# Head sums of a hybrid decoder layer: split in two halves over all rows, or fp32 in four strips and spread through DRAM

## The chip, the core and the metric

The kernel runs on one core of a Trainium2 chip. The metric is the device time of one execution in microseconds (us). One matmul instruction multiplies a stationary operand (at most 128 x 128) with up to 512 moving columns.

## The reference

One layer for 1088 tokens (1024 of a prompt and 8 sequences of 8), model width 1024. A projection of the normalised input gives the columns of two branches. The branch that matters here is RWKV-7: 512 channels are 8 heads of 64.

```python
kk = heads(k * lp["k_k"])
kk = kk * lax.rsqrt(jnp.sum(kk * kk, axis=-1, keepdims=True) + 1e-12)
...
y, wkv_new = wkv7_scan(wkv_prev.astype(f32), rh, heads(decay), kh, vh, kk, ah)
mean = jnp.mean(y, axis=-1, keepdims=True)
var = jnp.mean(jnp.square(y - mean), axis=-1, keepdims=True)
y = ((y - mean) * lax.rsqrt(var + GN_EPS)).reshape(B, T, MIX_WIDTH)
y = y * lp["ln_w"].astype(f32) + lp["ln_b"].astype(f32)
bonus = jnp.sum(rh * kh * lp["r_k"].astype(f32), axis=-1, keepdims=True) * vh
y = (y + bonus.reshape(B, T, MIX_WIDTH)).astype(pr.dtype) * g
```

Four sums run over the 64 channels of a head for each token: that of the key, the bonus, the mean and the variance. The branch is gated, projected, merged with a pooling branch, projected again and added to the input; a squared-ReLU MLP of width 4096 follows.

## The kernel before

Features lie on the partitions and the 1088 tokens along the free axis, so a unit f (0 to 3) of 128 partitions holds two heads. A sum over a head is a sum over 64 partitions: a matmul with a constant 128 x 128 matrix of two blocks of ones (`bones`), which gives the sum on all 64 rows of the head at once.

Two phases. In the first, a long stream of matmuls (the input projection, then the pooling branch's output projection, `op_job`) fills TensorE. Each product is made of three fp32r matmuls, high by high, high by low and low by high, in chunks of 364, 362 and 362 columns (tiles `whi`, `wlo` for weights, `hx` for rows). Beside the stream run generators: `heads` (line 1650), which takes the four units one after the other, `chains`, `pools` and `or_rows`. `heads` does for each unit:

- `front` (1112): squares the key, sums it over the head, takes the inverse root, and makes decays and keys;
- `scores`, then `inverse`, `level` and `affine`: small matmuls and VectorE work;
- beside these `bonus` (1214) of this unit, and `post` (1561) of the unit before: group norm (mean, variance), bonus and gate. `post` of the last unit has no unit behind it and runs at the end, in pieces; it uses plain fp32 matmuls with the constant in `kct`.

The second phase begins with `or_job` (1900), which multiplies the rows that all four `post` calls have left; its first products need those of `post(3)`.

Before each step a generator yields `need(...)`: it goes on when the planner's own clock (`Clocks`, line 80, fed with a modelled cost of each operation) says that the operands are there. This writes TensorE's order down once and for all. `Ledger` (184) then sets the order of VectorE and of SP's queue from a second model. Every engine takes its instructions in that order and waits for semaphores.

A head sum outside the last `post` is taken so: `halves` splits the row into a high part (ScalarE, a copy to fp32r) and a low part (VectorE, a subtraction), `sums` multiplies both with `bones` into one PSUM bank, chunk by chunk (512, 288, 288 in `front`, 364, 362, 362 elsewhere). `rinv` and `inv` add epsilon and take a reciprocal of all the chunk's columns on VectorE, with the root on ScalarE. Rows are tiles `wt`, a ring of five.

Of the kernel before, what the change touches and what calls it, by code (L numbers as in the profile page):

```python
# [183 lines left out]
class Ledger:  # L184
# [44 lines left out]
    def product(self, shape, n, dtype):  # L229

        if dtype == F32R:
            return n / 2.4 + 14
        if shape == (32, 32):
            return 22
        if max(shape) <= 64:
            return max(58, 0.78 * n + 11)
        if shape == (128, 32):
            return 0.47 * n
        if shape == (128, 128):
            return max(207, 1.62 * n + 60)  # L240
        return max(58, 1.05 * n)
# [302 lines left out]
class K:  # L544
# [42 lines left out]
    def took(self, n, mode):  # L587
        if not self.clocks.on:
            return max(n / 0.6 * min(mode) / 128, 30) + 3
        if mode == (64, 128):  # L590
            return n + 10
        if mode == (64, 64):
# [238 lines left out]
    def inv(self, ps, n, out, scale, eps):  # L831
        nc = self.nc
        nc.scalar.activation(out, ps[:, :n], AF.Identity, bias=self.eps[:, eps:eps + 1], scale=scale)
        for a in range(0, n, 182):
            nc.vector.reciprocal(out[:, a:min(a + 182, n)], out[:, a:min(a + 182, n)])

# [275 lines left out]
    def front(self, f):  # L1112
# [14 lines left out]
        hi, lo = (self.row(self.p1, "wt", 5, F32R) for _ in range(2))  # L1127
        for c0, n in FH:
            self.halves(kk[:, c0:c0 + n], hi[:, c0:c0 + n], lo[:, c0:c0 + n])
        for c0, n in FP:  # L1130
            yield self.need(hi[:, c0:c0 + n], lo[:, c0:c0 + n], wait=0)
            self.rinv(self.sums(hi[:, c0:c0 + n], lo[:, c0:c0 + n]), n, kk[:, c0:c0 + n], 1.0, 1)
        t1, tha = self.wt(hi), self.wt(lo)
        for c0, n in FP:
# [6 lines left out]
            nc.scalar.activation(tha[:, c0:c0 + n], ps[:, :n], AF.Tanh, bias=self.hp[:, 4 + f:5 + f], scale=0.5)  # L1141
        yield X(f)
# [43 lines left out]
        q = [self.wt(x, F32R) for x in (t1, tha)]  # L1186
        self.halves(k, *q)
        v = self.wt(k)
        nc.sync.dma_start(v, self.d_x[8 + f])
        self.cur.update(q=q, v=v)  # L1190
# [23 lines left out]
    def bonus(self, f, d):  # L1214

        nc, (hi, lo), v, bv = self.nc, d["q"], d["v"], self.wt(d["kk"])
# [344 lines left out]
    def post(self, f):  # L1561
# [57 lines left out]
        else:  # L1619
            hi, lo = (self.row(self.p1, "wt", 5, F32R) for _ in range(2))  # L1620
            for c0, n in CH:
                self.halves(y[:, c0:c0 + n], hi[:, c0:c0 + n], lo[:, c0:c0 + n])
            for c0, n in CH:
                s = slice(c0, c0 + n)
                yield self.need(hi[:, s], lo[:, s], wait=0)
                nc.vector.scalar_tensor_tensor(y[:, s], self.sums(hi[:, s], lo[:, s]), -1.0 / 64, y[:, s], op0=ALU.mult, op1=ALU.add)
                nc.scalar.activation(sq[:, s], y[:, s], AF.Square)
                self.halves(sq[:, s], hi[:, s], lo[:, s])
            yield self.need(hi, lo, wait=0)
            for c0, n in CH:  # L1630
                s = slice(c0, c0 + n)
                yield self.need(hi[:, s], lo[:, s], wait=0)
                self.inv(self.sums(hi[:, s], lo[:, s]), n, sq[:, s], 1.0 / 64, 2)
            nc.scalar.activation(sq, sq, AF.Sqrt)
            for c0, n in CH:
                s = slice(c0, c0 + n)
                nc.vector.tensor_tensor(y[:, s], y[:, s], sq[:, s], op=ALU.mult)
                nc.scalar.activation(y[:, s], y[:, s], AF.Identity, bias=self.par("ln_b", f), scale=self.par("ln_w", f))
            yield self.need(y[:, 0:1], banks=(), wait=0)
            bv, sg = yield from gate(sq, hi)  # L1640
# [62 lines left out]
    def run(self):  # L1703
        tc, nc, io = self.tc, self.nc, self.io
        with ExitStack() as ctx:
# [3 lines left out]
            dp = ctx.enter_context(tc.tile_pool(name="dp", bufs=1, space=DRAM))  # L1709
# [799 lines left out]
```

## Time and profile before

| | us |
|---|---|
| runs (3), median | 1580.98 (1580.57 to 1582.55) |
| profiled execution, its own time | 1581.41 |
| its span, first to last instruction | 1579.6 |
| TensorE busy | 1529.0 (97%) |
| VectorE busy | 1106.4 (70%) |
| ScalarE busy | 661.6 (42%) |

TensorE is busy nearly all the time; the time before its first matmul is about 9 us. In the rows below, PE is TensorE, DVE VectorE, ACT ScalarE, SPq the queue of DMAs that SyncE issues. A matmul row gives its start, its length with the pipeline's fill, and how many instructions it merges; an fp32 matmul leaves two records, an fp32r matmul one. Matmuls overlap, so their price is read from start to start.

### The profile page before, as it was taken

To read this page: it belongs to the slowest core of one execution; us is meant where nothing else is said; L and a number is where in the kernel's file an instruction comes from. 1 tells how busy PE (TensorE), PEld (TensorE's weight loads), DVE (VectorE), ACT (ScalarE), POOL (GpSimd) and SP (SyncE) were. 2 spreads that over 40 slices of the span, in tenths; PEclk is the share of its full clock that TensorE was granted. 3 is DMA by queue.
4 is the path that set the end of the run, shared out by engine and by line. 5 is a ranking of instruction groups with operands and counts; after the bars stand their busy time and mean duration, and the time that the engine had idled before them with its cause. 6 is when DMAs were issued, how large, how long until landed. Compare 5 with 4: busy or idle time off the path is not lost.

```text
span 1579.6 us, 34105 instructions
## 1 busy us (share of the span) xinstructions
PE 1529.0 (97%) x13822; PEld 1430.2 (91%) x13822; DVE 1106.4 (70%) x1945; ACT 661.6 (42%) x1294; POOL 141.4 (9%) x231
## 2 busy tenths in 40 slices
PE   6999899999999999999999999999999999999997
PEld 2998788887898889888899999999999999999997
DVE  5486568777777658546535798999667796666776
ACT  5554364365336434423223572222334344334552
POOL 2100100000000000113401210000000050000000
PEclk9999999999999999999999999999999999999999
DMA  9242524344324334854875565665436996664754
GB/s 368 83 124 94 187 65 122 106 124 136 109 86 154 104 125 145 311 184 173 307 272 183 183 200 182 228 232 178 150 139 238 391 356 196 203 197 156 229 171 152
DMA packets 136493, 290.04 MB, mean 184 GB/s; under 512 B 36976, under 2 KB 41072, under 8 KB 136336
## 3 DMA queue, kind: packets, MB, share of 16 engines
q1 hardware_dynamic: 129952, 266.75, 49.3%
q10 hardware_dynamic: 4320, 14.00, 2.5%
q0 software_dynamic: 2064, 7.13, 1.4%
q8 instruction: 108, 1.77, 0.5%
q14 instruction: 49, 0.40, 0.1%
HBM read 210.54 MB, written 77.28 MB: 182 GB/s over the span
## 4 chain that ended last, share of the span: by engine, by line
PE 58%; DVE 5%; DMA 4%; ACT 1%; issue 1%; POOL 0%; SPq 0%; DVEq 0%; ACTq 0%; POOLq 0%
PE mm L581 38%; PE wc L581 12%; PE w L581 8%; DVE wt L400 2%; DMA mg<-in_w_ff 1%; DVE hx L400 1%; DVE wlo L400 1%; DMA wt<-d_bv 1%; DMA hid<-in_w_ada_mlp 1%; DVE mg L400 0%; DMA wt<-d_x 0%; DVE hv L400 0%; ACT wt L400 0%; POOL t L400 0%; DMA t<-d_th 0%
## 5 line engine op out<-in xcount | busy, mean ns | idle before, releaser
L581 PE MATMUL mm<-hx,whi 128*128 128x362 f32 (+2 forms) x2944 | 687.8, 321 | 7.1 <-ACT px L400 2.7
L581 PEld LDWEIGHTS mm<-hx,whi 128*128 128x128 f32 x2944 | 495.3, 189 | 29.2 <-issue 8.0
L581 PE MATMUL mm<-hx,wlo 128*128 128x362 f32 (+2 forms) x1472 | 462.1, 314 | 2.4 <-issue 2.4
L581 PEld LDWEIGHTS mm<-hx,wlo 128*128 128x128 f32 x1472 | 278.4, 189 | 3.8 <-issue 3.5
L581 PE MATMUL mm<-mg,whi 128*128 128x272 f32 (+2 forms) x1312 | 248.7, 288 | 0.2 <-ACT t L400 0.2
L581 PEld LDWEIGHTS mm<-mg,whi 128*128 128x128 f32 x1312 | 205.4, 188 | 4.8 <-issue 2.5
L581 PE MATMUL mm<-mg,wlo 128*128 128x272 f32 (+2 forms) x656 | 188.5, 287 | 0.0
L581 PE MATMUL wc<-hx,whi 128*128 128x272 f32 x896 | 170.5, 288 | 0.0
L400 ACT ACTIVATE whi<-hid 128x512 fp32r<-128x512 f32 x128 | 80.4, 630 | 150.1 <-PE mm L581 54.9
L581 PEld LDWEIGHTS wc<-hx,whi 128*128 128x128 f32 x896 | 140.3, 188 | 0.2 <-issue 0.2
L581 PE MATMUL wc<-hx,wlo 128*128 128x272 f32 x448 | 128.9, 288 | 1.8 <-DVE wlo L400 1.8
L581 PEld LDWEIGHTS mm<-mg,wlo 128*128 128x128 f32 x656 | 123.5, 188 | 0.0
L400 DVE TENSOR_TENSOR wlo<-hid,whi 128x512 fp32r<-128x512 f32 x128 | 87.4, 686 | 45.2 <-ACT whi L400 44.3
L400 DVE TENSOR_TENSOR wlo<-wraw,whi 128x512 fp32r<-128x512 f32 x84 | 59.5, 709 | 61.2 <-ACT whi L400 61.0
L581 PE MATMUL w<-hx,whi 128*128 128x272 f32 (+1 forms) x480 | 98.1, 298 | 1.6 <-ACT hx L400 1.5
L400 ACT ACTIVATE whi<-wraw 128x512 fp32r<-128x512 f32 x100 | 62.5, 627 | 66.5 <-PE mm L581 24.2
L400 POOL TENSOR_TENSOR hx<-hx,rs 128x64 f32<-128x64 f32 x24 | 36.5, 1523 | 565.9 <-DVE rs L400 556.6
L581 PEld LDWEIGHTS wc<-hx,wlo 128*128 128x128 f32 x448 | 84.2, 188 | 2.2 <-DVE wlo L400 2.2
L581 PEld LDWEIGHTS w<-hx,whi 128*128 128x128 f32 x480 | 77.7, 189 | 3.0 <-ACT hx L400 1.8
L581 PEld LDWEIGHTS mm<-mg,hx 128*128 128x128 f32 x576 | 72.8, 188 | 5.0 <-issue 5.0
L581 PE MATMUL mm<-mg,hx 128*128 128x272 f32 (+2 forms) x576 | 74.7, 289 | 0.0
L581 PE MATMUL w<-hx,wlo 128*128 128x272 f32 (+1 forms) x240 | 70.7, 296 | 0.8 <-DVE wlo L400 0.8
(292 smaller groups left out, 2277.7 us busy)
## 6 DMA issues: line engine op xcount, KB each, us to landing
t<-d_t SPq DMA_DIRECT2D x56, 544.0 KB, 5.1
hid<-in_w_ff SPq DMA_DIRECT2D x110, 256.0 KB, 4.1
d_t<-hx SPq DMA_DIRECT2D x102, 272.0 KB, 2.2
hid<-in_w_ff SPq DMA_DIRECT2D x42, 512.0 KB, 3.9
wraw<-in_w_in SPq DMA_DIRECT2D x68, 256.0 KB, 2.9
mg<-in_w_ff SPq DMA_DIRECT2D x58, 256.0 KB, 5.3
hid<-in_w_ada_mlp SPq DMA_DIRECT2D x24, 512.0 KB, 5.9
d_th<-px SPq DMA_DIRECT2D x22, 544.0 KB, 3.1
```

The source lines that it names most:

```text
L400: r = f(*a, **kw)
L581: r = self.nc.tensor.matmul(out, lhsT, rhs, **kw)
```

## The change

All head sums but those of `post(3)` are taken in fp32 from the row itself. `strips` cuts the 1088 columns in four strips of 272. For each strip one matmul with 32 columns of `bones` (16 of each head) writes 32 partitions of one bank, at four places of the array. The result, 128 x 272, goes through ScalarE (with root and scale, or copied), for key and variance through one VectorE reciprocal of 272 columns; then `fan` stores every 16th partition (8 x 272) to DRAM and loads it back twice, broadcast to the 64 partitions of each head, over the row that was summed. The splits, and the loops over chunks around the sums, are gone; the element-wise work after the mean runs over whole rows. Two modelled costs are added for the planner.

```diff
+    def strips(self, x):
+        n = x.shape[1] // 4
+        ps = self.ps("w")
+        for i in range(4):
+            self.mm(ps[32 * i:32 * i + 32, :n], self.kc("bones")[:, 48:80], x[:, i * n:(i + 1) * n], start=True, stop=True, tile_position=(0, 32 * i))
+        return ps[:, :n]
+    def invert(self, x, eps, scale):
+        nc, r = self.nc, x[:, :HALF // 2]
+        nc.scalar.activation(r, self.strips(x), AF.Sqrt, bias=self.eps[:, eps:eps + 1], scale=scale)
+        nc.vector.reciprocal(r, r)
+        self.fan(x)
+    def fan(self, x):
+        nc, d = self.nc, self.dp.tile([8, HALF // 2], F32, name=self.nm("d_n"))
+        nc.sync.dma_start(d, x[0:P:16, :HALF // 2])
+        for h, hs in enumerate(HB):
+            nc.sync.dma_start(x[hs].rearrange("p (i n) -> p i n", i=4), d.rearrange("(i h) n -> h i n", h=2)[h:h + 1].broadcast_to([64, 4, HALF // 2]))
...
     # front: the key
-        hi, lo = (self.row(self.p1, "wt", 5, F32R) for _ in range(2))
-        for c0, n in FH:
-            self.halves(kk[:, c0:c0 + n], hi[:, c0:c0 + n], lo[:, c0:c0 + n])
-        for c0, n in FP:
-            yield self.need(hi[:, c0:c0 + n], lo[:, c0:c0 + n], wait=0)
-            self.rinv(self.sums(hi[:, c0:c0 + n], lo[:, c0:c0 + n]), n, kk[:, c0:c0 + n], 1.0, 1)
+        yield self.need(kk, wait=0)
+        self.invert(kk, 1, 1.0)
...
     # bonus
-        for c0, n in CH:
-            s = slice(c0, c0 + n)
-            yield self.need(hi[:, s], lo[:, s], wait=0)
-            nc.vector.tensor_tensor(bv[:, s], self.sums(hi[:, s], lo[:, s]), v[:, s], op=ALU.mult)
+        yield self.need(q, wait=0)
+        nc.scalar.activation(q[:, :HALF // 2], self.strips(q), AF.Copy)
+        self.fan(q)
+        yield self.need(q, banks=(), wait=0)
+        nc.vector.tensor_tensor(bv, q, v, op=ALU.mult)
...
     # post(0) to post(2): mean, then variance
+            nc.scalar.activation(sq[:, :HALF // 2], self.strips(y), AF.Copy, scale=-1.0 / 64)
+            self.fan(sq)
+            yield self.need(sq, banks=(), wait=0)
+            nc.vector.tensor_tensor(y, y, sq, op=ALU.add)
+            nc.scalar.activation(sq, y, AF.Square)
+            yield self.need(sq, wait=0)
+            self.invert(sq, 2, 1.0 / 64)
```

In the built program 84 matmuls with `bones` are gone and 56 strip matmuls stand there (14 sums of four), with 14 stores and 28 loads of `fan`. The order on TensorE moves too. First the key sum of unit 0 on TensorE, before: high and low part (`wt_735`, `wt_736`) follow each other for 512 and for 288 columns between matmuls of the stream (`mm`); the pair of the last 288 columns stands 15 matmuls further on.

```order
L581 MATMUL mm_840<-hx_216,whi_818 128x362
L581 MATMUL mm_840<-hx_215,wlo_819 128x362
L581 MATMUL w_901<-wt_735,bones 128x512
L581 MATMUL w_901<-wt_736,bones 128x512
L581 MATMUL w_908<-wt_735,bones 128x288
L581 MATMUL w_908<-wt_736,bones 128x288
L581 MATMUL mm_838<-hx_217,whi_818 128x364
L581 MATMUL mm_838<-hx_218,whi_818 128x364
```

The same sum in the change, one row for the four strips of `wt_731`:

```order
L583 MATMUL mm_834<-hx_214,whi_812 128x362
L583 MATMUL mm_834<-hx_213,wlo_813 128x362
L583 MATMUL w_886<-wt_731,kct 32x272 x4
L583 MATMUL mm_832<-hx_215,whi_812 128x364
L583 MATMUL mm_832<-hx_216,whi_812 128x364
L583 MATMUL mm_832<-hx_215,wlo_813 128x364
```

The sum stands nine matmuls of the stream earlier, and the three pairs are one group. Where SP's queue takes `post(0)` before (`wt_3897` gets the gate row, `wt_3898` the bonus):

```order
L400 DMA d_opl_86<-d_3284 128x1088
L400 DMA wt_3897<-d_x_119 128x1088
L400 DMA wraw_3800<-in_w_in 128x512
L400 DMA wt_3898<-d_bv_66 128x1088
L400 DMA d_th_91<-px_3684 128x1088
L400 DMA wraw_3955<-in_w_in 128x512
L400 DMA wraw_4099<-in_w_in 128x512
```

The same place in the change, where `d_n` is the small DRAM tile of a `fan`, for the mean first, then for the variance:

```order
L402 DMA wt_4027<-d_x_119 128x1088
L402 DMA wt_4028<-d_bv_66 128x1088
L402 DMA d_n_3547<-wt_3494 8x272
L402 DMA wraw_3838<-in_w_in 128x512
L402 DMA wt_3494<-d_n_3547 64x4x272 x2
L402 DMA d_th_91<-px_3671 128x1088
L402 DMA wraw_3941<-in_w_in 128x512
L402 DMA d_n_3768<-wt_3494 8x272
L402 DMA wt_3494<-d_n_3768 64x4x272 x2
```

Between the store of `d_n` and its loads stands a weight load (`wraw`) for the mean and nothing for the variance; the loads of a weight stand behind those of `d_n`. Of the 14 `fan`s seven have a DMA of another kind between store and loads. Last, the end of `heads` on TensorE before: the last variance sum of `post(3)` (a wide fp32 matmul with `kct`), then the second phase, whose first product with a chunk in a tile `w` is `or_job(0)`'s.

```order
L581 MATMUL mm_8331<-hx_7394,whi_8253 128x362
L581 MATMUL mm_8331<-hx_7392,wlo_8254 128x362
L581 MATMUL w_8389<-wt_8159,kct 128x362
L581 MATMUL mm_8448<-hx_7396,whi_8420 128x364
L581 MATMUL mm_8448<-hx_7398,whi_8420 128x364
L581 MATMUL mm_8448<-hx_7396,wlo_8421 128x364
L581 MATMUL mm_8449<-hx_7396,whi_8420 128x362
L581 MATMUL mm_8449<-hx_7398,whi_8420 128x362
L581 MATMUL mm_8449<-hx_7396,wlo_8421 128x362
L581 MATMUL w_8450<-hx_7396,whi_8420 128x362
```

And in the change:

```order
L583 MATMUL mm_7934<-hx_7763,whi_7860 128x364
L583 MATMUL mm_7934<-hx_7761,wlo_7861 128x364
L583 MATMUL w_7940<-wt_7734,kct 128x362
L583 MATMUL mm_7935<-hx_7761,whi_7860 128x362
L583 MATMUL mm_7935<-hx_7763,whi_7860 128x362
L583 MATMUL mm_7935<-hx_7761,wlo_7861 128x362
```

From the last row of `post(3)` to the first row of `or_job(0)` in a tile `w` it is 7 rows before and 220 in the change, all matmuls of the stream. On their own between stream matmuls stand 14 groups of the recurrence's matmuls (`wc` from `S` and `ra`) before and 5 in the change; of the 14 strip groups 4 stand alone and 10 beside other small matmuls.

## Rows read from the trace of the kernel before

**Rows 1.** The page, part 1: busy time (us, share, instructions) of each engine.

```profile
PE 1529.0 (97%) x13822; PEld 1430.2 (91%) x13822; DVE 1106.4 (70%) x1945; ACT 661.6 (42%) x1294; POOL 141.4 (9%) x231
```

**Rows 2.** Busy time in stretches: us, PE, PEld, DVE, ACT, POOL, granted clock, DMA.

```profile
80.00:730.00 650.00, 628.04 (x6879) 561.56 (x6877) 454.65 (x830) 287.75 (x611) 43.39 (x116) 1.00 0.41 135
```

**Rows 3.** Waits of PE from 80 to 732 us: total, times, longest.

```profile
PE w L581 <- DVE wt L400: 2.4, 4, 1.5
```

**Rows 4.** Instructions that read tile bones, and idle time before them (us, times).

```profile
L581 PE MATMUL w<-wt,bones x84: 293/328/497, 83.8 to 635.5; 128*128 128x362 f32 x40, 128*128 128x364 f32 x20, 128*128 128x288 f32 x16, 128*128 128x512 f32 x8
...
  DVE wt L400: 6.0, 8
```

**Rows 5.** Timeline of PE: start, length, instructions; two places with bones.

```profile
529.41 0.63 PE L581 MATMUL w<-wt,bones 128*128 128x512 f32 x2
529.88 0.50 PE L581 MATMUL mm<-hx,whi 128*128 128x362 f32 x2
...
614.35 0.49 PE L581 MATMUL mm<-hx,whi 128*128 128x362 f32 x2
...
614.85 0.52 PE L581 MATMUL w<-wt,bones 128*128 128x362 f32 x2
615.20 0.49 PE L581 MATMUL mm<-hx,whi 128*128 128x364 f32 x2
```

**Rows 6.** Timeline of PE: four 128x32 fp32 matmuls of 512 columns in the stream.

```profile
36.33 0.65 PE L581 MATMUL mm<-hx,whi 128*128 128x364 f32 x3
36.91 1.07 PE L581 MATMUL wc<-aw,sT 128*32 128x512 f32 x8
37.90 0.77 PE L581 MATMUL mm<-hx,wlo 128*128 128x364 f32 x3
38.51 0.33 PE L581 MATMUL mm<-hx,whi 128*128 128x364 f32 x1
```

**Rows 7.** Timeline of PE: four strips of 272 columns at the start.

```profile
16.38 0.67 PE L581 MATMUL w<-sq,even 128*32 128x272 f32 x8 [0.66 <-ACT sq L400]
```

**Rows 8.** Timeline of PE: a wide fp32 product in the stream.

```profile
698.56 0.32 PE L581 MATMUL mm<-hx,wlo 128*128 128x362 f32 x1
698.72 0.77 PE L581 MATMUL w<-wt,kct 128*128 128x364 f32 x2
...
699.65 0.33 PE L581 MATMUL mm<-hx,wlo 128*128 128x364 f32 x1
```

**Rows 9.** Timeline of PE: a group of the recurrence alone in the stream.

```profile
566.47 0.32 PE L581 MATMUL mm<-hx,wlo 128*128 128x362 f32 x1
566.72 0.27 PE L581 MATMUL wc<-S,ra 64*64 64x64 f32 x2
...
567.43 0.33 PE L581 MATMUL mm<-hx,wlo 128*128 128x364 f32 x1
```

**Rows 10.** Timeline of PE: where the second phase begins.

```profile
728.92 0.32 PE L581 MATMUL mm<-hx,wlo 128*128 128x362 f32 x1
730.73 1.00 PE L581 MATMUL w<-hx,whi 128*128 128x362 f32 x2 [1.49 <-ACT hx L400]
731.57 0.33 PE L581 MATMUL w<-hx,wlo 128*128 128x362 f32 x1
```

**Rows 11.** Groups of VectorE by shape: busy us, mean ns, idle before.

```profile
L400 DVE RECIPROCAL wt<-wt 128x182 f32<-128x182 f32 x32 | 39.1, 1250 | 4.0 <-ACT wt L400 3.8
L400 DVE RECIPROCAL r<-r 128x272 f32<-128x272 f32 x1 | 1.9, 1854 | 10.4 <-ACT r L400 10.4
L400 DVE TENSOR_TENSOR wt<-wt,wt 128x1088 fp32r<-128x1088 f32 x7 | 9.2, 1317 | 4.0 <-ACT wt L400 3.9
```

**Rows 12.** Waits of SP's queue from 80 to 732 us: total, times, longest.

```profile
SPq L400 <- DVE wlo L400: 221.1, 48, 13.7
```

**Rows 13.** DMAs: count, size, median us from issue to landing.

```profile
d_y<-y SPq DMA_DIRECT2D x3, 32.0 KB, 2.8
...
hx<-d_t SPq DMA_DIRECT2D x10, 272.0 KB, 3.7
```

More of the change, by code (lines that the diff above doesn't have):

```diff
@@ L238, in product @@
             return 0.47 * n
+        if shape == (32, 128):
+            return max(58, 0.68 * n)
         if shape == (128, 128):
@@ L591, in took @@
             return n + 10
+        if 32 in mode and P in mode:
+            return max(40, 0.6 * n)
         if mode == (64, 64):
@@ L1126, in front @@
             nc.scalar.activation(kk[:, c0:c0 + n], k[:, c0:c0 + n], AF.Square, scale=self.par("k_k", f))
-        hi, lo = (self.row(self.p1, "wt", 5, F32R) for _ in range(2))
-        for c0, n in FH:
-            self.halves(kk[:, c0:c0 + n], hi[:, c0:c0 + n], lo[:, c0:c0 + n])
-        for c0, n in FP:
-            yield self.need(hi[:, c0:c0 + n], lo[:, c0:c0 + n], wait=0)
-            self.rinv(self.sums(hi[:, c0:c0 + n], lo[:, c0:c0 + n]), n, kk[:, c0:c0 + n], 1.0, 1)
-        t1, tha = self.wt(hi), self.wt(lo)
+        yield self.need(kk, wait=0)
+        self.invert(kk, 1, 1.0)
+        t1, tha = self.wt(), self.wt()
         for c0, n in FP:
@@ L1141, in front @@
             nc.scalar.activation(tha[:, c0:c0 + n], ps[:, :n], AF.Tanh, bias=self.hp[:, 4 + f:5 + f], scale=0.5)
+        yield self.need(kk, banks=(), wait=0)
         yield X(f)
@@ L1185, in front @@
         nc.vector.scalar_tensor_tensor(k, r, self.par("r_k", f), k, op0=ALU.mult, op1=ALU.mult)
-        q = [self.wt(x, F32R) for x in (t1, tha)]
-        self.halves(k, *q)
-        v = self.wt(k)
+        v = self.wt(t1)
         nc.sync.dma_start(v, self.d_x[8 + f])
-        self.cur.update(q=q, v=v)
+        self.cur.update(q=k, v=v)
     def ra(self, d, u):
@@ L1214, in bonus @@
     def bonus(self, f, d):
-        nc, (hi, lo), v, bv = self.nc, d["q"], d["v"], self.wt(d["kk"])
-        for c0, n in CH:
-            s = slice(c0, c0 + n)
-            yield self.need(hi[:, s], lo[:, s], wait=0)
-            nc.vector.tensor_tensor(bv[:, s], self.sums(hi[:, s], lo[:, s]), v[:, s], op=ALU.mult)
+        nc, q, v, bv = self.nc, d["q"], d["v"], self.wt(d["kk"])
+        yield self.need(q, wait=0)
[3 more added lines that the diff above has]
+        nc.vector.tensor_tensor(bv, q, v, op=ALU.mult)
         nc.sync.dma_start(self.d_bv[f], bv)
@@ L1619, in post @@
         else:
-            hi, lo = (self.row(self.p1, "wt", 5, F32R) for _ in range(2))
             for c0, n in CH:
[L1622 to L1638, printed above, removed]
+                yield self.need(y[:, c0:c0 + n], wait=0)
+            nc.scalar.activation(sq[:, :HALF // 2], self.strips(y), AF.Copy, scale=-1.0 / 64)
[5 more added lines that the diff above has]
+            self.invert(sq, 2, 1.0 / 64)
+            yield self.need(sq, banks=(), wait=0)
+            nc.vector.tensor_tensor(y, y, sq, op=ALU.mult)
+            nc.scalar.activation(y, y, AF.Identity, bias=self.par("ln_b", f), scale=self.par("ln_w", f))
             yield self.need(y[:, 0:1], banks=(), wait=0)
-            bv, sg = yield from gate(sq, hi)
+            bv, sg = yield from gate(sq, None)
             nc.vector.tensor_tensor(y, y, bv, op=ALU.add)
@@ L1708, in run @@
             self.hx = Pool(self.clocks, ctx.enter_context(tc.tile_pool(name="hx", bufs=1)))
-            dp = ctx.enter_context(tc.tile_pool(name="dp", bufs=1, space=DRAM))
+            dp = self.dp = ctx.enter_context(tc.tile_pool(name="dp", bufs=1, space=DRAM))
             scratch = lambda n, k: [dp.tile([P, NT], F32, name=f"{n}{i}") for i in range(k)]
```

## The prediction

> **What bounds the kernel now.** The page's busy times come first: TensorE works 97% of the span, VectorE 70%, ScalarE 42% [rows 1]. The stretch of the four units lies between about 80 and 730 us. There TensorE is busy 628.0 of 650 us, at a granted clock of 1.00, which is 2.4 GHz; VectorE has 454.7, so it has slack, and the DMA engines are busy 0.41 of the time [rows 2]. The reader is to see that a microsecond taken from TensorE in this stretch should move everything behind it, that no more than 22 us of idle time lie there, and that VectorE's work matters only where TensorE waits for its result. Of those waits the list has 2.4 us for tile `wt` of VectorE [rows 3].
>
> **What the change removes from TensorE.** 84 matmuls with `bones` [rows 4]. They stand in the stream with no gap of their own: a pair of 512 columns holds it from 529.41 to 529.88, 0.47 us, and a pair of 362 from 614.85 to 615.20, 0.35 us [rows 5]. Three matmuls of the stream run from 614.35 to 614.85, 0.166 us each [rows 5], so a `bones` matmul costs what one of these does. A sum of 2 x 1088 columns thus costs 1.0 us, and 14 sums 14.0 us.
>
> **What it adds.** 14 groups of four strips, two records each. The trace has the same group with 512 columns [rows 6]. From 36.33 to 38.51 us lie 2.18 us, with six stream matmuls of 0.166: the group holds the stream for 1.19 us, more than the 0.99 from its start to that of the next matmul, since entering and leaving cost too. The span of the group shrinks from 1.07 to 0.67 us with 272 columns [rows 6, 7], so I take 0.40 off: 0.79 us for a strip group alone. From start to start it is 0.99 of the 1.19; the other 0.20 is way in and out, which a group shares that stands beside other small matmuls, 0.59 us. In the new order 4 groups stand alone and 10 do not: 4 x 0.79 + 10 x 0.59 = 9.1 us. Bounds: all share, 8.3; none, 11.1. The direct gain is 14.0 - 9.1 = 4.9 us.
>
> A rule of the Trainium skill (TensorEngine Tiling (Array Packing), Theoretical Speedup) gives up to four times for a stationary side of at most 32. A full-width fp32 product of 364 columns takes 1.09 us less three stream matmuls, 0.60 us, here [rows 8]. By the rule a sum would be a quarter of three of these, 0.45 us, 14 of them 6.3 and the gain 7.7 us; I take the rows' 9.1, since the same page (Key Properties) says that a change of tiling mode drains the array, which the row of 1.19 us holds and the rule's factor leaves out.
>
> **The order.** A group of the recurrence alone in the stream costs 0.96 us less three stream matmuls, 0.46 [rows 9]; nine fewer stand alone. If each of these now shared its way with a neighbour, up to 9 x 0.46 = 4.1 us would go; nothing if other pieces are torn apart instead. I take 2 us.
>
> **Waits.** Before the `bones` matmuls the trace lists 6.0 us idle for VectorE's `wt`, 8 times, matmul and weight load counted together [rows 4]; on the matmul's side alone it is 2.4 [rows 3]. I take 4.5. Of 42 points where TensorE had to meet a chunk 14 are left, but three of them, the variance sums, have a `fan` ahead. Its price: a store of 32 KB lands after 2.8 us, a load of 272 KB after 3.7 [rows 13]; with the second load's issue, about 7 us. No TensorE instruction reads a `fan`'s result directly. Behind it come a VectorE pass of 1088 columns (1.32 us [rows 11]) and, for the variance, ScalarE's square, then strips. The written order leaves 45 to 81 stream matmuls and two small groups there, 10 to 16 us, which should cover about 10. Bounds for the new waits: nothing, or 3 us at each of the three variance sums; I take 2.5. So waits give 2.
>
> Where the second phase begins, TensorE stands from 728.92 to 731.57, 2.65 us for three stream matmuls, waiting for ScalarE's copy of the last `post` [rows 10]. In the new order 220 rows, not 7, lie between the last sum of `post(3)` and there, 213 x 0.166 = 35 us of cover. The stall of 2.1 us goes. Should that cover be lost, 2.1 come back.
>
> **Other engines.** VectorE loses its long reciprocals: 39.1 us in the largest group, 32 of 182 columns [rows 11], out of some 50 for seven sums, against seven of 272 at 1.9, 13 us; and the splits at 1.32 us a row [rows 11], 14 of them, 18 us. That is 55 us of 455, and it is what pulls the units forward in the order. It costs TensorE nothing by itself: the stream hides it, unless VectorE was late, which the waits above hold.
>
> SP's queue gets 42 DMAs. At a `fan` it waits for the store to land before the loads go out; a weight load stands behind. These have time: SP waits 221 us in 48 cases for `wlo`, that is, for a weight buffer to come free [rows 12], so loads go out early, and a half of weights feeds 36 matmuls, 6 us. I cost this at nothing; what hides it is that second buffer, and it costs up to 2.8 us a time if it is not there.
>
> **Sum.** 4.9 + 2 + 2 + 2.1 = 11.0 us. Against it I set 1.5 us for late landings in the front of a unit, where VectorE meets `kk` in a fixed order (bounds 0 and 4 x 1.5). 1581.4 - 9.5 gives 1571.9 us. The profiled execution (1581.4, its span 1579.6 and 1.8 around it) lies 0.4 above the median of 1581.0; I say 1572.
>
> **Rivals.**
> *The trips through DRAM cost the stream (slower).* The mechanism: SP stands at the loads until the store has landed, and the weight load behind it is late, so TensorE starves. Against: in this stretch the list of TensorE's waits has none for `wlo`; for: seven `fan`s have the store and loads back to back, with a weight load behind them. Each case costs up to 2.8 us, and from four of fourteen on (11 us) it decides. With seven: 1581.4 - 9.5 + 20 = 1592.
> The Trainium skill (DMA: Bandwidth & Descriptors, Anatomy of one DMA) says that a wait for a semaphore is taken by the issuing sequencer before dispatch; by that rule all that is queued on SP stands behind each `fan`, and SP's 221 us agree that it waits in order.
> *The gain goes into new waits (no change).* Everything in the stretch is ordered anew, and its 22 us of idle time are drawn again. If the new order is as much worse as the old was lucky, by 8 or 9 us, the time is 1580. For: those 22 us are more than twice the gain. Against: VectorE has less to do.
> *More is gained.* The 55 us less on VectorE remove other waits, say half of the remaining 15, and the regrouping brings its whole 4.1: 1581.4 - 9.5 - 7.5 - 2.1 = 1562.
>
> **How the numbers follow.** Changes within 0.2%, 3.2 us, can't be told from none. The forecast (4 to 14 us gained) gets 0.53, the larger gain 0.14, no change 0.17, the DRAM rival and what else is slower 0.16. Faster 0.67 with the first two, same 0.17, slower 0.16. The forecast's own range is 1567 to 1577; to leave out no more than 2 in 10 I go from 1562, the larger gain's time, to 1583, a little past no change.
>
> **What would show it.** Strip groups at 0.6 to 0.8 us of the stream each; no stall at the start of the second phase; the last `post` some 35 us ahead of it; TensorE's idle time in the stretch of the units at or under 20 us. It would be wrong if TensorE waited for `wlo` there, if strip groups held the stream for 1 us, or if waits at variance strips came to more than 5 us.

## The result, and the profile after

The changed kernel takes 1590.9 us (median of 6 runs, 1585.32 to 1593.36) against 1580.78 of the kernel before on the same chips (6 runs): ratio 1.0058, 95% interval 1.0039 to 1.0078. It is slower by about 9 us where 9 us less were forecast (1572). The profiled execution took 1591.0 us, its span 1589.2.

The page, part 1, of the changed kernel answers to [rows 1]:

```profile
PE 1531.4 (96%) x13850; PEld 1426.8 (90%) x13850; DVE 1055.4 (66%) x1856; ACT 633.7 (40%) x1240; POOL 149.4 (9%) x231
```

VectorE has lost 51 us, where 55 were reckoned; TensorE, which should have lost 5, has gained 2. The stretch of the units, which is 7.9 us longer now, against [rows 2] (same columns); at the 2800th matmul of the stream, behind the start of the second phase, the changed kernel is 5.7 us later:

```profile
80.00:737.90 657.90, 630.75 (x6907) 559.03 (x6906) 405.93 (x745) 260.75 (x559) 47.73 (x116) 0.98 0.46 145
```

Idle time has grown from 22.0 to 27.2 us, and the granted clock has fallen from 1.00 to 0.98. The list of TensorE's waits from 80 to 745 us (total, times, longest) answers to [rows 3]:

```profile
PE w L583 <- ACT wt L402: 14.5, 6, 4.8
...
PE mm L583 <- DVE wlo L402: 0.2, 1, 0.2
```

The first line was 1.0 us before. 13.3 of its 14.5 us are strip groups that wait for the row that they sum (6.8 at two variances, 6.2 at the keys of units 2 and 3, 0.2 at the key of unit 0); the rest is a product of `front`. The last line shows that weights are not late. One strip group that waits for nothing, on the timeline of TensorE (rows of the stream around it):

```profile
311.05 0.32 PE L583 MATMUL mm<-hx,wlo 128*128 128x362 f32 x1
311.30 0.67 PE L583 MATMUL w<-wt,kct 128*32 128x272 f32 x8
311.90 0.60 PE L583 MATMUL mm<-hx,whi 128*128 128x362 f32 x2
312.33 0.33 PE L583 MATMUL mm<-hx,wlo 128*128 128x362 f32 x1
```

From 311.05 to 312.33 lie 1.28 us with three stream matmuls of 0.166: 0.78 us for the group, to be read against [rows 4 to 6]. The prediction had 0.79. Three groups that do wait, for the variance of `post(0)`, the key of unit 3 and the variance of `post(2)`; the number in brackets is the idle time ahead of the row:

```profile
326.80 0.91 PE L583 MATMUL w<-wt,kct 128*32 128x272 f32 x8 [2.95 <-ACT wt L402]
...
521.99 1.79 PE L583 MATMUL w<-wt,kct 128*32 128x272 f32 x8 [4.85 <-ACT wt L402]
...
622.52 1.14 PE L583 MATMUL w<-wt,kct 128*32 128x272 f32 x8 [3.86 <-ACT wt L402]
```

The same eight records last 0.67 us above and 1.79 here. The stretches of 2 us around the second show why (the third number from the right is the granted clock):

```profile
518.00:520.00 2.00, 0.00 (x0) 0.00 (x0) 0.93 (x1) 0.00 (x0) 0.31 (x1) 1.00 0.92 229
...
522.00:524.00 2.00, 2.00 (x16) 0.65 (x16) 0.00 (x0) 0.72 (x2) 0.00 (x0) 0.50 0.13 48
...
526.00:528.00 2.00, 2.00 (x9) 2.00 (x8) 1.56 (x1) 0.97 (x1) 0.00 (x0) 0.50 0.00 0
528.00:530.00 2.00, 2.00 (x11) 1.34 (x9) 0.00 (x0) 0.00 (x0) 0.00 (x0) 0.88 0.01 4
```

TensorE stands for 4.85 us, and when it goes on it has 0.50 of its clock (1.2 GHz) up to 528 us. In the whole stretch of the units the clock is at that level for 27 us, before for 3.4 (sums over such stretches).

**Why the variance of `post(2)` waits.** ScalarE has the mean at 608.56 (608.18 and 0.38). Then SP's queue and VectorE's addition:

```profile
607.30 0.74 SPq L402 DMA_DIRECT2D wt<-d_x  x1
608.15 0.41 SPq L402 DMA_DIRECT2D wt<-d_bv  x1
608.66 0.60 SPq L402 DMA_DIRECT2D d_n<-wt  x1
609.83 0.32 SPq L402 DMA_DIRECT2D d_th<-px  x1
611.87 0.33 SPq L402 DMA_DIRECT2D wraw<-in_w_in  x1
614.53 1.26 SPq L402 DMA_DIRECT2D wt<-d_n  x2
...
619.99 1.29 DVE L402 TENSOR_TENSOR wt<-wt,wt 128x1088 f32<-128x1088 f32 x1 [5.82 <-DMA wt<-d_n]
```

The trip takes 11.4 us. Between store and load stand a store that waits for ScalarE and a weight load that waits for its buffer; the load goes out 5.9 us after the store. Where nothing holds it up (8 of the 14 trips) it is 1.7 to 1.9 us. What ended last here is not SP's other work, which it has issued by 612.3: then it stands for the store of 8.5 KB itself. SP's waits from 608 to 615 us (total, times, longest):

```profile
SPq L402 <- DMA d_n<-wt: 2.2, 1, 2.2
```

It is so at all three means, where the loads go out 5.4, 6.3 and 5.9 us after the store, SP standing 0.9, 2.7 and 2.2 us for it at the end. The other eleven stores have landed 1.7 to 1.8 us after their issue. Only the three have two loads of 544 KB (gate row and bonus) right ahead of them in the queue, as the rows show; that these loads hold the store up fits all 14 trips, but no run was made for it alone.

**Why the key of unit 3 waits.** ScalarE's square of `k` waits for its load, which SP issues behind a store of the last `post`:

```profile
513.56 0.34 SPq L402 DMA_DIRECT2D d_orh<-wt  x1
513.95 1.33 SPq L402 DMA_DIRECT2D wt<-d_x  x2
...
521.22 1.39 ACT L402 ACTIVATE wt<-wt,part 128x512 f32<-128x512 f32 x2 [4.66 <-DMA wt<-d_x]
```

Before, that chain was the same (a load of `k` behind the store of the last `post`, its row there 7 us after its issue), but the key's sums stood further on. Counted in the written order of TensorE, from the last product of the gate in `post` to the key's first product:

```
                      stream matmuls between   start to start ahead of the key's group, us
                      unit 2   unit 3          unit 2   unit 3
before                  63       78            under 0.9 both
changed                 24       30             1.7      5.4
variance later          18       30             8.0      5.7
var. and key later      24       54            10.8      1.2
order of 0.15 us        15       27            13.1      5.8
order of 0.45 us        24       30             5.8      5.2
rows spread on PE       24       21             6.2      9.0
post as before          60       48            under 0.9 both
key far                 75       69            under 0.9 both
```

(The rows below the second are experiments; ordinary is some 0.25 us.) From 48 matmuls on no wait is over 1.2 us; 24 go with waits from 1.7 to 10.8, so the distance alone does not set the wait. The splits on ScalarE and VectorE, and the two rows that they filled, stood in the chain that the planner saw; without them the sums stand 39 and 48 stream matmuls, 6.5 and 8 us, closer to the gate. Which of the two made how much of that is not shown. The planner's `Clocks` gives DMAs no queue and prices this load at 4.5 us and a whole trip of a `fan` at 5.3, so it knows neither that the load stands behind a store nor that it lands 7 us after its issue.

The stall at the start of the second phase [rows 10] is gone: ScalarE's last copy for `hx` ends at 705.1, the first product with a chunk in a tile `w` runs at 734.0 without a wait.

### The profile page after: what moved, and what is told of

It reads as the page before. It is cut to its first block, busy times and chain, and to the rows that moved or that the text cites. A ratio compares the mean times of both kernels' runs of the same rounds, so it can differ in the third digit from the quotient of the medians.

```text
span 1589.2 us, 34127 instructions
## 1 busy us (share of the span) xinstructions
PE 1531.4 (96%) x13850; PEld 1426.8 (90%) x13850; DVE 1055.4 (66%) x1856; ACT 633.7 (40%) x1240; POOL 149.4 (9%) x231
## 3 DMA queue, kind: packets, MB, share of 16 engines
q8 instruction: 109, 1.79, 0.5%
## 4 chain that ended last, share of the span: by engine, by line
PE 69%; DMA 12%; DVE 12%; issue 3%; ACT 3%; SPq 1%; POOL 0%; DVEq 0%; ACTq 0%; POOLq 0%
PE mm L583 46%; PE w L583 11%; PE wc L583 11%; DVE hx L402 3%; DMA wt<-d_n 2%; DMA hid<-in_w_ff 2%; DVE wt L402 2%; DVE hv L402 1%; DMA wt<-d_x 1%; DVE wlo L402 1%; SPq L402 1%; DMA d_n<-wt 1%; DVE bk L402 1%; DMA mg<-in_w_ff 1%; DMA aw<-in_w_ada_mix 1%
## 5 line engine op out<-in xcount | busy, mean ns | idle before, releaser
L402 POOL TENSOR_TENSOR hx<-hx,rs 128x64 f32<-128x64 f32 x24 | 39.9, 1662 | 567.3 <-DVE rs L402 544.3
```

What stands on the lines that cost most here:

```text
L402: r = f(*a, **kw)
```

## The experiments

Theory at first: *late trips*, the order gives a trip through DRAM too little time, TensorE stands at strips, and the clock falls. Rivals: *SP held* (rival of the prediction), and *redraw*: whatever makes the planner write another order loses, since the order of before is a fortunate one. Most edits below make the planner write a new order of TensorE as well. It stays row for row as it was only with the trips on another queue, the trips left out, and half or more of the sums; `k` loaded first moves four rows.

### Strip groups later

```diff
-            yield self.need(sq, wait=0)
+            yield self.need(sq, wait=0, spare=6000)
             self.invert(sq, 2, 1.0 / 64)
```

> Only the three variance strip groups are written later: the condition ahead of them asks for 6 us beyond the planned time of the square instead of 0.3. Theory 'late trips': the order was written with a trip through DRAM at some 5 us, the trace of the changed kernel shows about 11 us from the mean's copy to the addition, so TensorE stands 3.1 and 4.1 us at two variance groups and runs at half clock for 3.4 and 6.8 us behind them. The groups move by 27, 12 and 18 stream matmuls (4.5, 2.0 and 3.0 us); those waits fall from 7.2 to about 1 us and the two half-clock stretches go (about 4 us): 10 us faster than the changed kernel, ratio to before 0.999 to 1.001. Rival 'SP held' (the fans' waits on SP make weights and rows late): no change from the changed kernel, ratio 1.005 to 1.007. Rival 'redraw' (any new order loses about as much, whatever waits are taken away): the waits go but others of like size come, ratio 1.004 to 1.008.

Measured: 1.0132 (1.0115 to 1.0149). With the key's `need` given the same 6000:

> As the run with later variance groups, and the four key groups later by the same 6 us. Late trips: the key groups' waits (1.7 and 5.4 us, for a row of k whose load lands late) go too, with the 6.8 us of half clock behind the longer one (3.4 us lost): 8 to 10 us more, ratio to before 0.992 to 0.996, which is what the prediction had said of the change. Redraw: 1.002 to 1.008. SP held: 1.004 to 1.007.

Measured: 1.0133 (1.0118 to 1.0148). The variance waits shrink in the first (to 1.3 and 1.6 us) and go in the second, but the key of unit 2 waits 8.0 and 10.8 us: with the variance later, the tail of `post` is later too, and `k` is loaded behind it. So no theory's number came; waiting at one strip group had been hiding a wait at the next.

### The trips on another queue

In `fan`:

```diff
-        nc.sync.dma_start(d, x[0:P:16, :HALF // 2])
+        nc.gpsimd.dma_start(d, x[0:P:16, :HALF // 2])
```

and the two loads likewise.

> The 42 DMAs of the fans are issued from GpSimd's queue instead of SP's; TensorE's order is the same row for row. SP held: rows and weights behind the fans come earlier, the key groups' waits (1.7 and 5.4 us) and other late landings shrink, ratio 0.998 to 1.001. Late trips: the trip itself is shorter where loads stood on SP behind a weight load or a store that waits (store at 608.66 us, loads only at 614.53), so the two variance waits shrink from 7.2 to about 2 us and the half clock with them, while the key waits stay: 6 to 9 us faster than the changed kernel, ratio 1.000 to 1.002. Redraw: TensorE's order being the same, no more than 2 us either way, ratio 1.004 to 1.007.

Measured: 1.0157 (1.0142 to 1.0172). The timeline of GpSimd for the mean of `post(0)`:

```profile
319.17 0.56 POOL L402 DMA_DIRECT2D d_n<-wt  x1 [6.65 <-ACT wt L402]
326.32 1.26 POOL L402 COPY z<-iv 32x32 f32<-32x32 f32 x4 [6.59 <-DVE iv L402]
...
328.22 1.24 POOL L402 DMA_DIRECT2D wt<-d_n  x2
```

Here the loads go out 9 us after the store, behind copies that wait for VectorE, and the variance waits 7.8 us. At the mean of `post(2)` GpSimd has nothing left ahead of the loads and still stands for the store:

```profile
622.07 0.56 POOL L402 DMA_DIRECT2D d_n<-wt  x1 [9.07 <-ACT wt L402]
...
628.64 1.25 POOL L402 DMA_DIRECT2D wt<-d_n  x2 [2.71 <-DMA d_n<-wt]
```

This store lands 6.3 us after its issue, that of `post(1)` after 6.0, as long as from SP's queue; SP has issued the two loads of 544 KB some 1.5 and 0.7 us ahead of each of them. So the trip did not become shorter at the means on a queue of its own, and SP, freed of the trips, gave nothing back: the key groups still wait 2.5 and 5.3 us. No expected time came. With TensorE's order the same this run is 16 us slower than the changed kernel; its stretch of the units has 41 us of half clock against 27.

### Parts undone

The key as before (the piece `front: the key` of the diff reversed):

> The key's sum as before (split halves and matmuls of 128 x 128 in pieces); bonus, mean and variance as changed. Late trips: the two key waits (7.1 us) and the half clock behind them (3.4 us) go, the variance waits (7.2) and theirs stay; the key's direct gain is lost (4 of 14 sums, 1.4 us): 8 to 9 us faster than the changed kernel, ratio 1.000 to 1.001. Strip price (a strip group costs the stream more than the 0.8 us reckoned): a third of any excess would go, less than 2 us, ratio 1.004 to 1.006. Redraw: 1.003 to 1.008.

Measured: 1.0211 (1.0196 to 1.0225), the reverse of what was expected: in yet another order TensorE waits 19.7 us for ScalarE's `wt`, 14.5 of them at three variance groups. The row of `k` loaded ahead of that of `wa`, in units 1 to 3:

```diff
-        wa = self.wt()
-        nc.sync.dma_start(wa, self.d_x[12])
+        if f == 0:
+            wa = self.wt()
+            nc.sync.dma_start(wa, self.d_x[12])
         yield X(4 + f)
-        k, kk = self.wt(), self.wt()
+        k = self.wt()
         nc.sync.dma_start(k, self.d_x[4 + f])
+        if f:
+            wa = self.wt()
+            nc.sync.dma_start(wa, self.d_x[12])
+        kk = self.wt()
```

> In units 1 to 3 the row of k is loaded ahead of the row of decay and gate inputs instead of behind it; TensorE's order differs in four rows. Late k (the key groups wait for a load that lands 7 us after a late issue): k lands 1 to 3 us earlier, the key waits fall from 7.1 to 3 or 4 us, with less half clock: ratio 1.001 to 1.004. If the load stands behind the store of the last post and that decides: unchanged, 1.005 to 1.007. Redraw: TensorE's order being almost the same, 1.004 to 1.008.

Measured: 1.0061 (1.0039 to 1.0084), unchanged: the key of unit 2 no longer waits, that of unit 3 still 4.2 us; both its loads stand behind the same store. So some 3 us less of waits brought nothing either. Mean and variance as before (the last piece of the diff reversed):

> Mean and variance as before (split halves, 128 x 128, in pieces); key and bonus as changed. Late trips: no trip stands in the chain of a post any more, so its tail and the next k are as early as before; 8 sums gain 0.35 us each: ratio 0.996 to 1.000. Redraw: 1.003 to 1.012, with waits of other kinds. Late k alone (the key's whole row against pieces): the key waits stay, 1.002 to 1.005.

Measured: 1.0044 (1.0026 to 1.0062). The key stands 60 and 48 matmuls behind the gate and does not wait; in its place the list has products `w`, among them those with `bones`, waiting for VectorE's `wt`:

```profile
PE w L583 <- DVE wt L402: 6.9, 4, 3.0
```

### The trips left out, in three orders

`post` plans its two trips but doesn't make them; the mean's addition reads the 272 columns four times. The expectations below name `bonus` too, but its trip is still made, in all three runs. Counted by tile `d_n`, stores of the changed kernel and of this run:

```profile
L402 SPq DMA_DIRECT2D d_n<-wt x14: 579/596/697, 88.2 to 627.5; - x14
...
L402 SPq DMA_DIRECT2D d_n<-wt x8: 580/601/692, 87.4 to 586.5; - x8
```

The eight are those of the four keys and the four bonuses; the six of mean and variance are gone.

```diff
-            self.fan(sq)
+            self.skip(sq)   # only self.clocks.op(...) of its three DMAs
```

> The trips through DRAM of bonus, mean and variance are left out (the rows are not spread, so those values are wrong), but still planned, so TensorE's order is row for row that of the changed kernel; the key keeps its trip. Late trips: the variance waits (7.2 us) and the half clock behind them go, the tail of a post comes some 20 us earlier, so the next unit's row of k can be loaded earlier and the key waits (7.1 us) shrink below 3: 12 to 20 us faster than the changed kernel, ratio to before 0.993 to 0.999. Rival 'redraw' (the written order of the kernel before is a fortunate one and any other loses some 10 us or more, trips or not): 1.003 to 1.010. Rival 'strip form' (the groups themselves cost more than reckoned): 1.004 to 1.007.

Measured: 1.0022 (1.0006 to 1.0038). Waits for ScalarE's `wt`, 14.5 us in the changed kernel:

```profile
PE w L583 <- ACT wt L402: 6.8, 3, 5.1
```

Of these 5.9 us are the keys of units 2 and 3 (0.8 and 5.1); no variance waits. So the key's wait of unit 3 does not hang on these trips, and the gain, some 6 us, is half of the least that was expected. The same in the two other orders of the changed kernel (below):

> The changed kernel in the order of 0.45 us, with the trips of bonus, mean and variance left out but still planned (the rows are not spread, so those values are wrong); TensorE's order is that of the run with 0.45 us row for row, whose ratio was 1.0107. Late trips: 0.003 to 0.008 below that, 1.003 to 1.008. Trips of no account: 1.009 to 1.013.

Measured: 1.0041 (1.0026 to 1.0056), against 1.0107.

> The same in the order of 0.15 us, whose ratio was 1.0215 with waits of 20 us at strip groups. Late trips: 0.004 to 0.012 below that, 1.009 to 1.018. Trips of no account: 1.019 to 1.024.

Measured: 1.0140 (1.0116 to 1.0163), against 1.0215. So with TensorE's order held row for row the trips of mean and variance cost 0.0036, 0.0066 and 0.0075, 6 to 12 us, each beyond the two intervals taken together. That part of *late trips* holds in all three. What the trips of key and bonus cost was not measured.

### The order itself

No part of the change; in the kernel before the planner asks for another spare time.

```diff
-    def need(self, *aps, banks=("w",), wait=1000, spare=300, slack=0):
+    def need(self, *aps, banks=("w",), wait=1000, spare=450, slack=0):
```

> A control without any of the change: the kernel before, in which the planner asks for 0.45 instead of 0.3 us of spare time ahead of each meeting, so that it writes another order of the same instructions. Redraw: slower by 5 to 15 us, ratio 1.003 to 1.010, with new waits and new half clock. Late trips: the loss belongs to the change, ratio 0.998 to 1.002.

Measured: 1.0081 (1.0059 to 1.0102), as *redraw* had it. With `spare=150`:

> A second control without the change: the kernel before, the planner asking for 0.15 instead of 0.3 us ahead of each meeting. Redraw (the order of the kernel before is a fortunate one): again slower, ratio 1.002 to 1.010. If the first control (1.008) was only an unlucky draw: 0.999 to 1.002.

Measured: 1.0022 (1.0005 to 1.0040), at the edge of both. Neither control equals before, though the second only just. The changed kernel with 450 and with 150:

> The changed kernel in another order: the planner asks for 0.45 us, as in the first control of before. Redraw: the changed kernel is one draw of many and costs about what the control of before costs in the like draw, ratio 1.000 to 1.010 against before, and not above the control's 1.008 by more than 0.002. Loss of the change's own (trips and late rows whatever the order): 1.010 to 1.018, some 10 us above the control.

Measured: 1.0107 (1.0083 to 1.0131), between the two: 4 us above the control.

> The changed kernel in a third order: the planner asks for 0.15 us, as in the second control. Redraw: within 0.003 of the second control's ratio, or below it, since the strips cost TensorE some 5 us less. Loss of the change's own: 0.005 or more above the second control.

Measured: 1.0215 (1.0187 to 1.0242), with the key's group 15 matmuls behind the gate. Over three planners' settings the kernel before has 1.000, 1.0081 and 1.0022, the changed kernel 1.0058, 1.0107 and 1.0215, and without the trips 1.0022, 1.0041 and 1.0140. A new order alone costs 3 and 13 us here, which is as much as the whole result. The changed kernel is above its control in each of the three, by 0.006, 0.003 and 0.019; the 0.003 is within the intervals. Without the trips of mean and variance it is 0.002 above its control, 0.004 below, and 0.012 above: what is left of the change has no fixed sign.

### TensorE's work, in the order of before

Half of each pair of `bones` left out, but planned:

```diff
-        for i, x in enumerate((hi, lo)):
-            self.mm(ps, self.bones, x, start=i == 0, stop=i == 1)
+        self.mm(ps, self.bones, hi, lo=lo, start=True, stop=True)   # lo is only planned
```

> The kernel before with the second matmul of each of its 42 pairs of sums left out (the low halves are not summed, so the sums are short of them); the planner still counts them, so every other row of TensorE, and VectorE's order but for a few rows, stands as it stood. Theory 'a microsecond is a microsecond' (the prediction's premise: what is taken from TensorE's stream in the units moves everything behind it): 42 x 0.166 = 7 us off, ratio 0.994 to 0.997. Rival 'waits fill it' (the order is so tight that other engines' results are then late): 0 to 3 us off, ratio 0.998 to 1.001.

Measured: 1.0053 (1.0035 to 1.0072): 7 us less work, and 8 us slower. Two stretches of this run, the units and a part of the last one, columns as in [rows 2]:

```profile
80.00:734.00 654.00, 627.70 (x6837) 559.20 (x6835) 454.69 (x831) 287.77 (x611) 42.06 (x116) 0.99 0.41 134
640.00:670.00 30.00, 25.89 (x375) 22.77 (x375) 12.97 (x19) 14.12 (x23) 2.92 (x4) 0.83 0.68 249
```

and the longest wait in the second, on its timeline of TensorE:

```profile
651.13 0.97 PE L584 MATMUL mm<-hx,whi 128*128 128x362 f32 x2 [3.82 <-DVE px L400]
```

The same stretch and the same wait in the kernel before:

```profile
640.00:670.00 30.00, 27.30 (x452) 24.33 (x451) 13.93 (x23) 15.82 (x29) 3.48 (x5) 0.94 0.80 282
```

```profile
649.60 0.60 PE L581 MATMUL mm<-hx,whi 128*128 128x362 f32 x2 [2.54 <-DVE px L400]
```

A third matmul added to each pair, unplanned:

```diff
-            self.mm(ps, self.bones, x, start=i == 0, stop=i == 1)
+            self.mm(ps, self.bones, x, start=i == 0, stop=False)
+        self.nc.tensor.matmul(ps, self.bones, lo, start=False, stop=True)
```

> The kernel before with a third matmul in each of the 42 pairs of sums (the low half added once more), not planned, so that every other row of TensorE keeps its place: 7 us more work. If TensorE's work sets the pace of the units: 1.004 to 1.005. If a chain through the other engines sets it, and the order only fills it: 0.999 to 1.002, the extra work lying where TensorE would have waited.

Measured: 1.0050 (1.0030 to 1.0070). Work added is paid in full. When the k-th matmul of the stream (those with `whi` or `wlo`) starts in the profiled execution, run less before, us:

```
k        before      half the sums   more sums
1400      376.4          +0.6          +4.8
2000      531.0          +0.3          +7.5
2400      628.3          +0.6          +7.1
2800      737.9          +4.3          +8.0
8000     1470.5          +7.2         +10.0
```

Up to the 2400th matmul, some 6 us of removed work bring nothing at all. The stretch up to there, in this run and before, and one part of it in this run (columns as in [rows 2]):

```profile
80.00:628.90 548.90, 528.49 (x5630) 471.93 (x5629) 396.02 (x730) 250.11 (x539) 29.11 (x96) 0.99 0.37 118
...
80.00:628.30 548.30, 531.08 (x5669) 475.96 (x5668) 395.70 (x730) 250.22 (x540) 30.43 (x96) 1.00 0.37 118
...
186.00:193.00 7.00, 7.00 (x84) 5.21 (x85) 0.72 (x1) 4.01 (x8) 0.59 (x1) 0.51 0.16 40
```

TensorE's idle time is 20.4 us there, before 17.2: it comes earlier to the next result of another engine and waits for it. The other half is the clock: behind a wait of 1.8 us it is at 0.50 for 6.9 us, in a stretch where before it stayed at 1.00. After the 2400th matmul TensorE stands longer in one place (3.82 against 2.54 us, for the same result of VectorE), half clock follows for 10.2 instead of 3.4 us, and from there on it is behind. So both theories of this run missed; the order is tight on both sides. Behind the 2800th matmul both runs lose 2 to 3 us more. There, at 740 to 765 us, VectorE takes some seven rows in another order in both than in the kernel before, so these 2 to 3 us may not be TensorE's work.

### Rows spread on TensorE

For mean and variance, four products of 32 x 128 with a constant instead of a trip:

```diff
+            self.mm(ps[:, :n], self.kc("wide")[q, :], r[q, :], start=True, stop=True, tile_position=(32 * i, 0))
...
+            yield from self.widen(sq[:, :HALF // 2], lambda s, ps: nc.vector.tensor_tensor(y[:, s], ps, y[:, s], op=ALU.add))
```

> In a post the rows of mean and variance are spread by four matmuls of 32 x 128 each (24 of 272 columns, about 6 us of TensorE in all) instead of a store and loads; key and bonus keep their trips. Late trips: about 8 us less in a post's chain each time, the variance waits go and k can be loaded earlier: ratio 0.998 to 1.003, below the changed kernel's 1.0058. Redraw alone: 1.004 to 1.012. If TensorE's work counts: 6 us are lost again, 1.004 to 1.007.

Measured: 1.0136 (1.0114 to 1.0158), in a new order and above every range. No mean or variance in strips waits over 2 us, yet tiles `wt` of ScalarE are waited for 19.3 us in all. The timeline of TensorE at the key of unit 3:

```profile
540.38 1.79 PE L584 MATMUL w<-wt,kct 128*32 128x272 f32 x8 [8.82 <-ACT wt L403]
```

### The key back at its distance

`spare=9000` in the key's `need`; in the second run the variance's 6000 as well.

> The changed kernel with only the key's groups written later (9 us beyond the planned time of the squares instead of 0.3): in units 2 and 3 they stand 75 and 69 stream matmuls behind the last product of a post's gate, against 24 and 30 in the changed kernel and 63 and 78 in the kernel before. Late k: their waits (1.7 and 5.4 us) and the half clock behind the longer one go; the variance waits stay: 7 to 10 us faster than the changed kernel, ratio 0.998 to 1.002. Redraw: 1.004 to 1.012, with waits of like size at other places.

Measured: 1.0128 (1.0114 to 1.0142).

> Both the key's groups later (9 us, so 69 stream matmuls behind the gate in units 2 and 3) and the variance groups (6 us). Late results as the cause: neither the key nor the variance waits are left, and what the prediction reckoned comes out: ratio 0.991 to 0.998. Redraw: 1.003 to 1.012.

Measured: 1.0095 (1.0079 to 1.0112). No key of units 2 and 3 waits in either, as *late k* had it. But in the first run TensorE stands at one variance group (`post(2)`) for 18.7 us. Its timeline, a row of TensorE, then SP and VectorE:

```profile
660.25 1.13 PE L583 MATMUL w<-wt,kct 128*32 128x272 f32 x8 [18.67 <-ACT wt L402]
...
632.59 0.60 SPq L402 DMA_DIRECT2D d_n<-wt  x1
633.36 0.32 SPq L402 DMA_DIRECT2D hx<-d_oph  x1
635.04 0.32 SPq L402 DMA_DIRECT2D hx<-d_opl  x1
...
644.73 1.32 SPq L402 DMA_DIRECT2D wt<-d_n  x2
...
657.72 1.29 DVE L402 TENSOR_TENSOR wt<-wt,wt 128x1088 f32<-128x1088 f32 x1 [15.38 <-DMA wt<-d_n]
```

Now the trip falls where SP fetches the rows of both branches for the next product: six of these loads (of 544 KB) stand between its store and its loads, 12.1 us, and the addition begins 13 us later. From the end of ScalarE's copy (630.4) to the addition it is 27 us. Three stretches of it, columns as in [rows 2], show the DMA engines full (the last two numbers) and the clock falling:

```profile
630.00:640.00 10.00, 8.91 (x220) 8.29 (x219) 4.20 (x5) 2.77 (x7) 2.81 (x6) 0.94 1.02 373
640.00:650.00 10.00, 0.84 (x74) 0.73 (x74) 0.72 (x1) 2.35 (x4) 0.00 (x0) 0.57 1.03 410
650.00:660.00 10.00, 0.00 (x0) 0.00 (x0) 1.29 (x1) 0.91 (x1) 0.54 (x1) 0.50 0.79 234
```

In the second run the group still waits 5.9 us. In the same first run the mean of `post(0)` has its bonus row behind the store, and the loads go out 1.8 us after it:

```profile
333.17 0.60 SPq L402 DMA_DIRECT2D d_n<-wt  x1
333.83 0.43 SPq L402 DMA_DIRECT2D wt<-d_bv  x1
334.94 1.26 SPq L402 DMA_DIRECT2D wt<-d_n  x2
```

So a DMA between store and loads costs nothing there, where two loads ahead of the store went with 5.4 us. No version beats the kernel before.

## Why the prediction was wrong, point by point

**The premise** that a microsecond taken from TensorE in the units moves everything behind it: this is the step that failed first. It was read from a busy share of 97% and a clock of 1.00. In the order of before, 7 us less work gave 8 us more time, and 7 us more work also gave 8. The busy share did not show that the order puts the stream's matmuls closely into the times of the other engines' chains: of the work taken out, up to the 2400th matmul, about half became waiting and half went into half clock.

**The price of the strips** was right where it could be read: 0.78 us alone against 0.79, and a `bones` matmul is worth 0.165. The price of a group beside small matmuls, 0.59, was not read by itself. TensorE's busy time in the units is 2.7 us longer, but 25 us of it ran at half clock, 3.4 before; at the full clock, an estimate, it would be 7 us shorter, which fits the 4.9 us with the 2 of the regrouping.

**The waits** had the wrong sign: 4.5 less 2.5 were to be won. On the rows for ScalarE's and VectorE's `wt` 11 us more are spent (14.5 where it was 1.0 and 2.4), though idle time as a whole grew by 5.2. Waits at variance groups came to 6.8 us; more than 5 was the prediction's own sign of being wrong. Two terms were off. A trip was priced at 7 us; it took 11.4 at `post(2)`, because the store, priced at 2.8 us, was not there before 5.4 to 6.3 us at the three means; the loads behind it land in 3.8 to 4.5 us where the trace has it, near the 3.7 reckoned. And the key's sums were given no price at all: 6.2 of the 14.5 us are theirs, since they moved from 63 and 78 to 24 and 30 matmuls behind the gate. That a DMA's wait for a semaphore is taken by the issuing sequencer before dispatch was in hand (the Trainium skill, DMA: Bandwidth & Descriptors, Anatomy of one DMA). The trace agrees: SP stands 2.2 us for the store of `post(2)` before it issues the loads. It was weighed for the weights behind a trip; what goes out ahead of the store was not looked at. The 1.5 us against late landings in the front of a unit can't be read apart.

**The clock** had no term. Rows of the stream at 1.2 GHz take 0.30 us for 0.166, so the 25 us that TensorE is busy at that level cost some 11 us, an estimate; before it was 3.4 us at that level.

**The regrouping** (2 us) can't be read apart. From the 250th to the 2800th matmul of the stream the changed kernel takes 5.2 us more. Of that, -4.9 is the strips', +4.3 idle time and some +8 more half clock (11 less the 3 of before, whose half clock behind its stall counts here), which leaves 2 or 3 us won by fewer groups. Redrawn orders make this number weak.

**The second phase's start** came nearly as said: no stall, and the last row is there 29 us ahead, where some 35 were forecast. Some 3 us are lost behind it: `ada_mlp` loads and VectorE's `t` are waited for 2.5 and 2.4 us, in before 1.3 and nothing. Why stays open.

**The rivals.** The slower one had nearly the time (1592), but by luck: its mechanism, weights late behind the trips, is absent, since weights are waited for 0.2 us. What it said of SP, that it stands until the store has landed, is true of the trip itself. The second rival, new waits in a new order, is what the controls show to be real: 3 and 13 us for a new order without any change, on either side of its price of 8 or 9.

What stays open: how the 9 us divide between the trips, the key's place and the luck of the order. The trips of mean and variance (6 to 12 us) and a new order (3 and 13 us) are each shown to be worth that much. The key's place is not: its waits are in the trace, but every run that moved the key's sums drew a new order too, and each wait taken away there came with another elsewhere.

## What to carry to other kernels

Before a microsecond of a busy engine is counted as won, leave that work out in the same order and look: here the kernel became 8 us slower. A change that makes a planner write a new order needs a control that redraws the order without the change; here both redrawn orders lost. A trip through DRAM in a chain costs what is on its way when its store goes out (1.7 us from store to load here, 5.4 to 6.3 behind two large loads, 12.1 among many), so it belongs where nothing large is issued just ahead of it and no in-order engine meets its result soon.

## What the runs showed of the hardware

A wait on TensorE can cost more than its length: behind 4.85 us of standing the granted clock was 0.50 for 6.8 us although the engine was busy at once, and behind 18.7 us it was 0.50 for 23.9 us, most of it the wait itself. With shorter waits it is not the same each time. The same row after the same wait of 2.2 us, in the changed kernel and in the run without the trips of mean and variance, each with the 4 us from 108 (the third number from the right is the granted clock):

```profile
108.41 0.80 PE L583 MATMUL mm<-hx,whi 128*128 128x362 f32 x2 [2.23 <-ACT px L402]
108.00:112.00 4.00, 3.59 (x12) 3.60 (x13) 2.85 (x5) 3.44 (x7) 1.31 (x4) 0.58 0.28 59
...
107.33 0.60 PE L583 MATMUL mm<-hx,whi 128*128 128x362 f32 x2 [2.23 <-ACT px L402]
108.00:112.00 4.00, 4.00 (x26) 4.00 (x25) 3.61 (x6) 2.36 (x5) 1.08 (x2) 1.00 0.20 66
```

With the key far TensorE stood 3.0 us up to 332.03 and kept 1.00. So with TensorE's order the same, one place can cost some 1.5 us more or less by the clock alone (half of 3.4 us, an estimate).

A store of 8.5 KB that was issued right behind two loads of 544 KB was followed by its dependent loads 5.4 to 6.3 us later; with nothing large ahead, and nothing else to hold the loads, it was 1.7 to 1.9. Issuing the store from GpSimd's queue, with the two loads still on SP's, did not change that (it landed after 6.0 and 6.3 us there). That the two loads are the cause was not tried by itself.
